# A projection with 512 instead of 256 moving columns per matmul, its end in halves

## The chip, the core and the metric

The kernel runs on one core of a Trainium2 chip. A core has TensorE (PE, matrix products; its loads of the stationary operand are listed as PEld), VectorE (DVE), ScalarE (ACT), GpSimd (POOL) and SyncE (SP, here the issuer of most DMA transfers). Operands lie in the on-chip memory SBUF, sums of matmuls in PSUM: 128 partitions, 8 banks of 512 float32 values each. The metric is the device time of one execution in microseconds (us). All numbers are float32; TensorE takes a weight and an activation as a pair of high and low parts each.

## The reference

A backbone with two layers over 512 tokens with 1024 features. Its last steps are what matters here: the channel mixer of the second layer, its gated residual, and the final RMSNorm.

```python
def conv_ffn(h, w_up, conv_w, conv_b, w_down):
    a, val = jnp.split(h @ w_up, 2, axis=-1)
    return (jax.nn.gelu(dwconv3(a, conv_w, conv_b), approximate=False) * val) @ w_down

def rms_norm(x, w):
    y = xf * lax.rsqrt(jnp.mean(xf * xf, axis=-1, keepdims=True) + EPS)
    return y * w

...
        x = x + gate_f[:, None, :] * conv_ffn(h, ...)
    return rms_norm(x, final_norm_w)
```

`w_down` is 2816 x 1024: 22 tiles of 128 rows (k = 0 to 21, FT = 22 in the kernel).

## The kernel before

The last projection computes, for four tiles i of 128 tokens, y = g @ w_down. The stationary operand is a 128 x 128 block of g (activations, high part gh or low part gl), the moving operand a k row block of the weights. Each product is three matmuls: gh with the high weights (line 1339), gl with the high weights (1340), gh with the low weights (1341). The 1024 output columns are done in four rounds j of 256 columns. In a round, four PSUM tiles, one for each token tile (tag acc, six banks), take the sums over all 22 k.

Weights come in loads of up to 8 k x 256 columns (1 MB) into two buffers (wraw). The class Weights converts them in sub-blocks of up to 4 k x 256 columns: ACT casts the high part (line 92), DVE subtracts for the low part (line 93), into three buffers each (whi, wlo). `get` hands out the next sub-block and converts one ahead; a cast waits until its buffer is free, that is until the matmuls of the sub-block three before it are done. In a round the sub-blocks begin at k0 = 0, 4, ..., 20; the last has 2 k.

The tiles of g lie in three pools: k = 0 to 5 in `gq` (high and low part side by side), the others in `zp` and `gp`.

After a round, `residual` adds the gated result to the residual stream xk: DVE multiplies the PSUM sum with the gate (line 1346) and adds it (1347), ACT squares it and sums the squares (1348). In the last round the last two sub-blocks are taken tile by tile: for each token tile the matmuls of both, its residual, then Ln and Exp for the inverse root (1370, 1371) and the scaling of the row: 256 columns with the final weights on DVE (1373), 512 on ACT (1374), 256 on DVE (1375). Two transfers write each tile out (1376 on ACT's queue, 1377 on SP's). Lines 1361 to 1363 do the first three quarters' share beforehand: the product with the final weights and the mean of the squares so far.

The order of an engine's instructions is not that of the program: the build reorders them, apart from pinned ones, by its own estimates of when each can run. It also adds all waits. The timelines show the order that runs. At the start of the stage 16 small matmuls that broadcast the gate (1324) and 32 transposes of the residual stream (1331) are mixed in.

The up-projection ahead of it (`group`) works with halves of a PSUM bank: `copy` (1176) reads one half of a bank while products for other banks, and then for the other half, follow. Its 512-column matmuls are on lines 288 to 290, with the weights stationary.

## Time and profile before

| | before |
|---|---|
| median of 3 runs | 1335.97 us (1333.49 to 1336.93) |
| profiled execution | 1333.99 us |
| its span | 1332.2 us |
| mean granted clock of TensorE | 0.995 |
| PE busy | 1304.5 us, 98% |
| PEld busy | 1147.6 us, 86% |
| DVE busy | 965.4 us, 72% |
| ACT busy | 625.2 us, 47% |
| instructions | 21229 |

The span is what the profile covers of the profiled execution; busy times are of its engines. A matmul's duration in a timeline (0.28 us for 256 columns) includes the passage through the array, which overlaps with the next one: the time that a matmul costs is the step from its start to the next start. A row of a timeline gives the start from the beginning of the span, the duration, engine, line and operation, output <- inputs, shapes, how many, and in brackets the idle time before it with what ended it.

### The profile page before, as it was taken

Reading aid. Unit: us, or ns where it says so; the run is one execution under the profiler, and the core shown is the slowest. Engines: PE = TensorE matmul, PEld = TensorE weight load, DVE = VectorE, ACT = ScalarE, POOL = GpSimd, SP = SyncE. Lnnn points to the kernel's source line nnn. Section 1 sums busy time; section 2 is a strip of 40 time slices with the busy share of each in tenths; the row PEclk is TensorE's granted clock in tenths of the full one; section 3 lists DMA queues with packets and bytes.
Section 4 is the critical chain, followed back from the end, with each engine's and each line's share of the span. In section 5 each row is a group of like instructions: output and inputs, shape, how many; then the busy total and the mean of one; then the engine's idle time right before and its main releaser. Section 6 shows DMA issues by size and latency. Waiting matters only on the chain. (4 is left out here: it accounts for less than half of the span.)

```text
span 1332.2 us, 21229 instructions
## 1 busy us (share of the span) xinstructions
PE 1304.5 (98%) x8456; PEld 1147.6 (86%) x8456; DVE 965.4 (72%) x1688; ACT 625.2 (47%) x1085; POOL 84.3 (6%) x87
## 2 busy tenths in 40 slices
PE   7999999999999999999999999999999999999997
PEld 4798888888779998889877898888999989899997
DVE  4668897887778878788766776667789897782333
ACT  4443445555545656565422253223456565663223
POOL 2204332311000000000000000000000000000000
PEclk9999999999999999999999999999999999999999
DMA  9842113674562122323466734555403423242231
GB/s 293 265 123 84 33 33 82 152 182 134 153 206 96 64 99 92 127 71 119 141 211 198 226 132 143 167 165 174 158 27 117 142 80 127 80 146 69 91 108 64
DMA packets 134995, 172.35 MB, mean 129 GB/s; under 512 B 14320, under 2 KB 103792, under 8 KB 129776
## 3 DMA queue, kind: packets, MB, share of 16 engines
q1 hardware_dynamic: 132896, 166.15, 39.3%
q10 hardware_dynamic: 2000, 4.85, 1.4%
q8 instruction: 66, 1.08, 0.3%
q14 instruction: 33, 0.27, 0.1%
HBM read 165.21 MB, written 2.10 MB: 126 GB/s over the span
## 5 line engine op out<-in xcount | busy, mean ns | idle before, releaser
L92 ACT CAST whi<-wraw 128x1024 fp32r<-128x1024 f32 (+1 forms) x122 | 124.1, 1021 | 280.8 <-PE pd L1340 70.4
L93 DVE TENSOR_TENSOR wlo<-wraw,whi 128x1024 fp32r<-128x1024 f32 (+1 forms) x122 | 145.2, 1192 | 107.7 <-ACT whi L92 107.1
L288 PE MATMUL p<-hf,whi 128*128 128x512 f32 (+1 forms) x640 | 215.4, 338 | 1.4 <-ACT whi L125 1.4
L290 PE MATMUL p<-hf,wlo 128*128 128x512 f32 (+1 forms) x640 | 214.6, 335 | 0.0
L289 PE MATMUL p<-hf,whi 128*128 128x512 f32 (+1 forms) x640 | 214.1, 335 | 0.0
L125 ACT CAST whi<-wraw 128x512 fp32r<-128x512 f32 (+1 forms) x160 | 113.0, 727 | 85.0 <-PE p L289 35.0
L290 PEld LDWEIGHTS p<-hf,wlo 128*128 128x128 f32 x640 | 120.1, 188 | 13.6
L288 PEld LDWEIGHTS p<-hf,whi 128*128 128x128 f32 x640 | 120.1, 188 | 12.3 <-ACT whi L125 1.6
L289 PEld LDWEIGHTS p<-hf,whi 128*128 128x128 f32 x640 | 120.1, 188 | 10.7
L126 DVE TENSOR_TENSOR wlo<-wraw,whi 128x512 fp32r<-128x512 f32 (+1 forms) x160 | 128.1, 817 | 0.9 <-ACT whi L125 0.5
L504 DVE SCALAR_TENSOR_TENSOR aa<-ar,sil,aa 128x512 f32<-128x512 f32 x140 | 104.8, 749 | 24.1 <-DMA ar<-in_ada_w_dram 21.8
L1339 PE MATMUL pd<-whi,g 128*128 128x256 f32 x352 | 98.2, 279 | 0.0
L1341 PE MATMUL pd<-wlo,g 128*128 128x256 f32 x352 | 98.1, 279 | 0.0
L1340 PE MATMUL pd<-whi,g 128*128 128x256 f32 x352 | 97.9, 278 | 0.0
L288 PE MATMUL pbd<-g,whi 128*128 128x512 f32 (+1 forms) x192 | 73.5, 383 | 0.0
L289 PE MATMUL pbd<-g,whi 128*128 128x512 f32 (+1 forms) x192 | 73.3, 382 | 0.0
L290 PE MATMUL pbd<-g,wlo 128*128 128x512 f32 (+1 forms) x192 | 73.1, 381 | 0.0
L288 PE MATMUL p<-T,whi 128*128 128x256 f32 x240 | 69.0, 288 | 0.0
L290 PE MATMUL p<-T,wlo 128*128 128x256 f32 x240 | 67.2, 280 | 0.0
L289 PE MATMUL p<-T,whi 128*128 128x256 f32 x240 | 67.2, 280 | 0.0
L1340 PEld LDWEIGHTS pd<-whi,g 128*128 128x128 f32 x352 | 66.3, 188 | 0.0
L1339 PEld LDWEIGHTS pd<-whi,g 128*128 128x128 f32 x352 | 66.1, 188 | 0.0
(679 smaller groups left out, 3296.3 us busy)
## 6 DMA issues: line engine op xcount, KB each, us to landing
ar<-in_ada_w_dram SPq DMA_DIRECT2D x160, 256.0 KB, 3.1
wraw<-in_upq_dram SPq DMA_DIRECT2D x40, 1024.0 KB, 4.8
wraw<-in_ffn_w_down_dram SPq DMA_DIRECT2D x16, 1024.0 KB, 5.3
wraw<-in_od_w_in_dram SPq DMA_DIRECT2D x12, 1024.0 KB, 5.6
wraw<-in_ev_w_in_dram SPq DMA_DIRECT2D x20, 512.0 KB, 5.2
araw<-in_ada_w_dram SPq DMA_DIRECT2D x16, 512.0 KB, 6.3
wraw<-in_ffn_w_down_dram SPq DMA_DIRECT2D x8, 768.0 KB, 4.7
wraw<-in_ev_w_out_dram SPq DMA_DIRECT2D x4, 1024.0 KB, 6.9
```

The lines of the kernel that those rows point to most:

```text
L92: self.nc.scalar.copy(hv, rv)
L93: self.pin(self.nc.vector.tensor_tensor(lv, rv, hv.bitcast(F32), ALU.subtract))
L125: self.nc.scalar.copy(hi, src)
L126: V.tensor_tensor(lo, src, hi.bitcast(F32), ALU.subtract)
L288: TE.matmul(o, wh, mh, start=start, stop=False, skip_group_check=True)
L289: TE.matmul(o, wh, ml, start=False, stop=False, skip_group_check=True)
L290: TE.matmul(o, wl, mh, start=False, stop=stop, skip_group_check=True)
L504: pin(V.scalar_tensor_tensor(self.acc[:], raw[:], sil[:, r, 0:1], self.acc[:], ALU.mult, ALU.add))
L1339: TE.matmul(o[i][:, 0:256], gh[:, ts], w[0][:, k - k0], start=k == 0, stop=False)
L1340: TE.matmul(o[i][:, 0:256], gl[:, ts], w[0][:, k - k0], start=False, stop=False)
L1341: TE.matmul(o[i][:, 0:256], gh[:, ts], w[1][:, k - k0], start=False, stop=k == FT - 1)
```

## The change

The last projection takes two rounds of 512 columns instead of four of 256. A load has up to 4 k x 512 columns, a sub-block 2 k x 512. A matmul moves 512 columns and fills a whole PSUM bank. In the second round the last two sub-blocks (k = 18 to 21) are done tile by tile and in two halves of 256 columns: for each half the matmuls of both sub-blocks, and then its residual; after the first half the sum of the squares so far and the product with the final weights for that half. `HALF` is the pair of slices 0:256 and 256:512.

```diff
-    for j in range(4):
-        plan += [wide(down[1], k0, k1, 256 * j) for k0, k1 in ((0, 8), (8, 16), (16, 22))]
+    for j in range(2):
+        plan += [([ktiled(down[1])[:, k0 : min(k0 + 4, FT), T * j : T * j + T]],
+                  [(0, s, s + 2, 0, T) for s in range(0, min(4, FT - k0), 2)]) for k0 in range(0, FT, 4)]
...
-    def down(o, w, i, k0):
+    def down(o, w, i, k0, c=slice(0, T)):
         ts = slice(i * P, (i + 1) * P)
-        for k in range(k0, min(k0 + 4, FT)):
+        for k in range(k0, k0 + 2):
             gh, gl = g[k]
-            TE.matmul(o[i][:, 0:256], gh[:, ts], w[0][:, k - k0], start=k == 0, stop=False)
-            TE.matmul(o[i][:, 0:256], gl[:, ts], w[0][:, k - k0], start=False, stop=False)
-            TE.matmul(o[i][:, 0:256], gh[:, ts], w[1][:, k - k0], start=False, stop=k == FT - 1)
+            TE.matmul(o[i][:, c], gh[:, ts], w[0][:, k - k0, c], start=k == 0, stop=False, skip_group_check=True)
+            TE.matmul(o[i][:, c], gl[:, ts], w[0][:, k - k0, c], start=False, stop=False, skip_group_check=True)
+            TE.matmul(o[i][:, c], gh[:, ts], w[1][:, k - k0, c], start=False, stop=k == FT - 1, skip_group_check=True)
...
+    def residual(o, i, j, c, n):
+        js = slice(j * T + c.start, j * T + c.stop)
+        t = fp.tile([P, T], F32, tag="t", name=f"yt{n}{i}", bufs=5)
+        V.tensor_tensor(t[:, c], o[i][:, c], gb[:, js], ALU.mult)
+        V.tensor_tensor(xk[i][:, js], xk[i][:, js], t[:, c], ALU.add)
+        S.activation(t[:, c], xk[i][:, js], AF.Square, accum_out=ss[:, i, n : n + 1])
...
-    subs = range(0, FT, 4)
-    for j in range(4):
+    subs = range(0, FT, 2)
+    for j in range(2):
...
-        V.tensor_tensor(xk[i][:, 0:768], xk[i][:, 0:768], fw[:, 0:768], ALU.mult)
-        V.tensor_reduce(ss[:, i, 4:5], ss[:, i, 0:3], axis=AX.X, op=ALU.add)
-        V.tensor_scalar(ss[:, i, 4:5], ss[:, i, 4:5], 1.0 / D, EPS, ALU.mult, ALU.add)
+        V.tensor_tensor(xk[i][:, 0:512], xk[i][:, 0:512], fw[:, 0:512], ALU.mult)
+        V.tensor_scalar(ss[:, i, 4:5], ss[:, i, 0:1], 1.0 / D, EPS, ALU.mult, ALU.add)
     w = [ws.get(), ws.get()]
     log_exp_table()
     for i in range(4):
-        for b in range(2):
-            down(o, w[b], i, subs[b - 2])
-        residual(o, i, 3)
-        S.activation(ss[:, i, 5:6], ss[:, i, 3:4], AF.Ln, scale=1.0 / D, bias=ss[:, i, 4:5])
+        for n, c in enumerate(HALF):
+            for b in range(2):
+                down(o, w[b], i, subs[b - 2], c)
+            residual(o, i, 1, c, 1 + n)
+            if n == 0:
+                V.scalar_tensor_tensor(ss[:, i, 4:5], ss[:, i, 1:2], 1.0 / D, ss[:, i, 4:5], ALU.mult, ALU.add)
+                V.tensor_tensor(xk[i][:, 512:768], xk[i][:, 512:768], fw[:, 512:768], ALU.mult)
+        S.activation(ss[:, i, 5:6], ss[:, i, 2:3], AF.Ln, scale=1.0 / D, bias=ss[:, i, 4:5])
```

## Rows read from the trace of the kernel before

**Rows 1.** The page, its first part: busy time of each engine, share of the span, instructions.

```profile
PE 1304.5 (98%) x8456; PEld 1147.6 (86%) x8456; DVE 965.4 (72%) x1688; ACT 625.2 (47%) x1085; POOL 84.3 (6%) x87
```

**Rows 2.** Groups by line and shape, 1160 to 1333 us: xcount | busy us, mean ns | idle before.

```profile
L1339 PE MATMUL pd<-whi,g 128*128 128x256 f32 x352 | 98.2, 279 | 0.0
...
L92 ACT CAST whi<-wraw 128x1024 fp32r<-128x1024 f32 x20 | 21.0, 1050 | 53.7 <-PE pd L1340 52.8 <-DMA wraw<-in_ffn_w_down_dram 0.9
...
L1363 DVE TENSOR_SCALAR ssf<-ssf 128x1 f32<-128x1 f32 x4 | 0.6, 149 | 0.0
```

**Rows 3.** The chain that ended last, in order of time: start us, us, what.

```profile
1327.73 0.48 DVE xk L1373
```

**Rows 4.** Timeline of PE, 256-column matmuls: start us, us, engine, line, operation.

```profile
1295.29 0.28 PE L1339 MATMUL pd<-whi,g 128*128 128x256 f32 x1
...
1299.61 0.28 PE L1339 MATMUL pd<-whi,g 128*128 128x256 f32 x1
...
1318.16 0.28 PE L1339 MATMUL pd<-whi,g 128*128 128x256 f32 x1
...
1324.85 0.28 PE L1341 MATMUL pd<-wlo,g 128*128 128x256 f32 x1
```

**Rows 5.** Busy time by stretch: sum PE, PEld, DVE, ACT, POOL, granted clock, DMA, GB/s.

```profile
1224.00:1228.00 4.00, 4.00 (x38) 4.00 (x37) 1.23 (x1) 1.05 (x1) 0.00 (x0) 1.00 0.55 190
1236.00:1240.00 4.00, 4.00 (x35) 4.00 (x34) 0.95 (x2) 0.96 (x5) 0.00 (x0) 1.00 0.33 118
```

**Rows 6.** Timeline of PE, 512-column matmuls of two other stages.

```profile
901.80 0.39 PE L288 MATMUL ppu<-hm,whi 128*128 128x512 f32 x1
...
905.70 0.40 PE L290 MATMUL ppu<-hm,wlo 128*128 128x512 f32 x1
...
1191.40 0.39 PE L288 MATMUL p<-hf,whi 128*128 128x512 f32 x1
...
1196.66 0.39 PE L290 MATMUL p<-hf,wlo 128*128 128x512 f32 x1
```

**Rows 7.** Timeline of PE where the last projection starts.

```profile
1199.97 0.47 PE L1324 MATMUL pgb<-dgb,ones 128*128 128x128 f32 x2
...
1202.56 0.61 PE L1324 MATMUL pgb<-dgb,ones 128*128 128x128 f32 x4
1202.92 0.36 PE L1339 MATMUL pd<-whi,g 128*128 128x256 f32 x1
...
1207.88 0.28 PE L1341 MATMUL pd<-wlo,g 128*128 128x256 f32 x1
```

**Rows 8.** Timeline of ACT in a group of the up-projection.

```profile
1180.30 0.35 ACT L1176 COPY R110r<-p 128x256 f32<-128x256 f32 x1
```

**Rows 9.** Timeline of PE beside it.

```profile
1180.78 0.31 PE L288 MATMUL p<-hf,whi 128*128 128x256 f32 x1
```

**Rows 10.** Timeline of DVE over the last two sub-blocks and behind.

```profile
1319.04 0.42 DVE L1346 TENSOR_TENSOR yt<-pd,gb 128x256 f32<-128x256 f32 x1 [6.19 <-PE pd L1341]
...
1321.07 0.48 DVE L1373 SCALAR_TENSOR_TENSOR xk<-xk,ssf,fw 128x256 f32<-128x256 f32 x1 [1.14 <-ACT ssf L1371]
1321.47 0.35 DVE L1375 TENSOR_SCALAR xk<-xk,ssf 128x256 f32<-128x256 f32 x1
...
1323.12 0.42 DVE L1346 TENSOR_TENSOR yt<-pd,gb 128x256 f32<-128x256 f32 x1 [0.51 <-PE pd L1341]
1323.75 0.49 DVE L1373 SCALAR_TENSOR_TENSOR xk<-xk,ssf,fw 128x256 f32<-128x256 f32 x1 [0.20 <-ACT ssf L1371]
...
1325.16 0.42 DVE L1346 TENSOR_TENSOR yt<-pd,gb 128x256 f32<-128x256 f32 x1 [0.33 <-PE pd L1341]
1325.62 0.43 DVE L1347 TENSOR_TENSOR xk<-xk,yt 128x256 f32<-128x256 f32 x1
```

**Rows 11.** Timeline of ACT behind the last matmul.

```profile
1326.00 0.72 ACT L1374 ACTIVATE xk<-xk,ssf 128x512 f32<-128x512 f32 x1
1326.63 0.40 ACT L1348 ACTIVATE yt<-xk 128x256 f32<-128x256 f32 x1
```

More of the change, by code (lines that the diff above doesn't have):

```diff
@@ L1333, in backbone @@
     ss = fp.tile([P, 4, 8], F32, tag="ss", name="ssf")
-    def down(o, w, i, k0):
+    def down(o, w, i, k0, c=slice(0, T)):
         ts = slice(i * P, (i + 1) * P)
-        for k in range(k0, min(k0 + 4, FT)):
+        for k in range(k0, k0 + 2):
             gh, gl = g[k]
-            TE.matmul(o[i][:, 0:256], gh[:, ts], w[0][:, k - k0], start=k == 0, stop=False)
-            TE.matmul(o[i][:, 0:256], gl[:, ts], w[0][:, k - k0], start=False, stop=False)
-            TE.matmul(o[i][:, 0:256], gh[:, ts], w[1][:, k - k0], start=False, stop=k == FT - 1)
-    def residual(o, i, j):
-        js = slice(j * 256, (j + 1) * 256)
-        t = fp.tile([P, 256], F32, tag="t", name=f"yt{j}{i}", bufs=5)
-        V.tensor_tensor(t[:], o[i][:, 0:256], gb[:, js], ALU.mult)
-        V.tensor_tensor(xk[i][:, js], xk[i][:, js], t[:], ALU.add)
-        S.activation(t[:], xk[i][:, js], AF.Square, accum_out=ss[:, i, j : j + 1])
-    subs = range(0, FT, 4)
-    for j in range(4):
+            TE.matmul(o[i][:, c], gh[:, ts], w[0][:, k - k0, c], start=k == 0, stop=False, skip_group_check=True)
[9 more added lines that the diff above has]
+    for j in range(2):
         o = [acc_t(f"pd1{j}{i}") for i in range(4)]
-        for k0 in subs if j < 3 else subs[:-2]:
+        for k0 in subs if j < 1 else subs[:-2]:
             w = ws.get()
@@ L1356, in backbone @@
                 down(o, w, i, k0)
-        if j < 3:
+        if j < 1:
             for i in range(4):
-                residual(o, i, j)
+                residual(o, i, j, slice(0, T), 0)
     for i in range(4):
-        V.tensor_tensor(xk[i][:, 0:768], xk[i][:, 0:768], fw[:, 0:768], ALU.mult)
-        V.tensor_reduce(ss[:, i, 4:5], ss[:, i, 0:3], axis=AX.X, op=ALU.add)
-        V.tensor_scalar(ss[:, i, 4:5], ss[:, i, 4:5], 1.0 / D, EPS, ALU.mult, ALU.add)
+        V.tensor_tensor(xk[i][:, 0:512], xk[i][:, 0:512], fw[:, 0:512], ALU.mult)
+        V.tensor_scalar(ss[:, i, 4:5], ss[:, i, 0:1], 1.0 / D, EPS, ALU.mult, ALU.add)
     w = [ws.get(), ws.get()]
```

## The prediction

> **What bounds the kernel now.** I read the share of busy time first, then the groups of lines, the chain that ended last, and then the timelines of the stretch that the change touches. TensorE (PE) is busy 98% of the span [rows 1]. The three matmul lines of the last projection, L1339 to L1341, have 352 instructions each, 1056 in all, and no idle time in front of them [rows 2]; so the stage is as long as its matmuls are, plus what runs behind the last one. The casts of its weights wait for PE (52.8 of 53.7 us of idle time), not the other way round [rows 2]: neither loads nor conversion bound it. The chain closes with the scaling of the fourth token tile on DVE at 1327.73 [rows 3], some 3 us behind the last matmul's start at 1324.85 [rows 4]. So two things count: time per moving column on PE, and the tail.
>
> The time per matmul has two levels. From 1318.16 to 1324.85 there are 59 steps of 0.1134 us; from 1295.29 to 1299.61 there are 36 steps of 0.120 us [rows 4]. DMA isn't the cause: a stretch with a DMA share of 0.55 has 38 matmuls in 4 us, one with 0.33 only 35, both at a granted clock of 1.00, the 2.4 GHz level [rows 5]. The two slow stretches lie just behind the start of the second and the fourth round. The slow steps last some 8 us of a round, as long as k = 0 to 5 take (72 x 0.120 = 8.6 us), and just these six tiles of the stationary operand lie in the pool `gq`. I take it that loading weights from there paces a 256-column matmul.
>
> **The change, part by part.**
>
> *Wider matmuls.* Removed: 1056 matmuls of 256 columns; 288 of them have k below 6: 288 x 0.120 + 768 x 0.1134 = 121.7 us. Added: 40 of the 44 pairs of round and k, each with 3 products for 4 tiles, are 480 matmuls of 512 columns, and the halves' 4 k x 3 x 4 x 2 are 96 of 256. The trace of before has no 512-column matmul with these operands (weights moving, activations stationary). The nearest rows are those of two other stages, with the operands exchanged: 17 steps in 3.90 us and 23 steps in 5.26 us, 0.2294 and 0.2287 us each [rows 6]. That is more than twice 0.1134, and less than twice 0.120. I take 0.2287: 480 x 0.2287 + 96 x 0.1134 = 120.7 us, a gain of 1.0 us. All of it comes from the slow k; the others lose a little. Bounds: if a matmul pays its columns at 2.4 GHz (256 columns are 0.1067 us) and a fixed 0.0067 us, which is what 0.1134 leaves, 512 columns take 0.2200 and the gain is 5.2 us. If the slow k stay slow at 2 x 0.120, the sum is 144 x 0.240 + 336 x 0.2287 + 10.9 = 122.3 us, a loss of 0.6 us.
>
> The Trainium skill (TensorE: Matmul & The Clock Gate, section "Back-to-back issue gap") gives a warm gap of N/2.4 + 2.5 ns, so 215.7 ns at 512 columns and 109.2 at 256. An estimate by that page makes the new stage 480 x 0.2157 + 96 x 0.1092 = 114.0 us, 7.6 us less than before, and a total of about 1328.2. The rows lie above it at both widths, by 4 and by 13 ns, so the trace doesn't bear it out here.
>
> *The start of the stage.* There 44 small matmuls (transposes and the broadcast of the gate) are mixed with the first ones of the projection: from 1199.97 to 1207.88 they and 16 of the projection's take 7.91 us. Four small ones take 0.36 us, from 1202.56 to 1202.92 [rows 7]. So 44 x 0.09 = 4.0 us, and the 16 take 3.9 us where 16 x 0.120 = 1.9 would do: 2.0 us go to changes of operation and to waits for the copies out of PSUM. A wider matmul in the same place does twice the work under the same wait. About half of the stretch has single ones in it, at most 9 x 0.11 = 1.0 us; I take 0.4 us of gain, with ends 0 and 1.0.
>
> *Weights.* Twelve loads stay twelve, with the same bytes. A sub-block is 2 k by 512 columns instead of 4 k by 256, so a conversion still has up to 1024 elements, and a sub-block lasts 24 x 0.2287 = 5.5 us against 48 x 0.1134 = 5.4. The short sub-blocks that ended each old round go. A 1024-wide cast takes 1.05 us [rows 2]; its subtraction on DVE is as wide. Nothing here is late; if the cover failed, one cast and one subtraction of some 2.3 us per sub-block would show as idle time of PE. At the one change of round left, 512-wide residuals stand in DVE's and ACT's queues ahead of at most one conversion: four tiles with two DVE operations of some 0.7 us (twice the columns of 0.42 [rows 10], less the fixed part) make 5.6 us, of which those of tile 3 alone, 1.4 us, and its square come behind the round's last matmul, with 5.5 us of matmuls to cover them. Two of the four new banks are free at once, and the other two wait for reads of tiles 0 and 1, which end their round 1.4 to 4 us earlier. I cost it at nothing.
>
> *The halves, a new wait.* In the last two sub-blocks a tile's first half is finished with 12 matmuls, L1346's successor reads it, and the second half's matmuls go on writing the same PSUM bank. Where before shows the same pattern, in the up-projection, the matmuls into one half of a bank start at 1180.78 [rows 9], behind the copy of the other half, which ends at 1180.30 + 0.35 [rows 8]: 0.13 us later. In the meantime PE does other products. No row shows one half read while PE writes the other. So I expect PE to wait. The price: after the last matmul's start at 1324.85 the next could start at 1324.96, but DVE's read starts only at 1325.16, takes 0.42 us [rows 4, 10], and 0.13 us follow: 1325.71, so 0.75 us for each wait. What is queued behind it on PE are the other tiles' matmuls; if they are put ahead, as in the up-projection, only tile 3 has nothing left to put ahead. I take one wait, +0.75 us; ends 0 and 4 x 0.75 = 3.0.
>
> The Trainium skill (PSUM — Partial Sum Buffer, section "PSUM bank collisions raise a hardware error") says that two engines must not touch the same bank and quadrant at once, even at different columns, and that the hardware doesn't arbitrate. By that rule the wait has to be there; it speaks against halves in one bank, and the trace agrees in the one place above.
>
> *The tail.* Per tile the halves add to DVE a product with the final weights (0.42), a second pair of multiply and add on the other half and a scalar step (0.15 [rows 2]). By durations a tile has 4 x 0.42 + 0.42 + 0.15 + 0.48 + 0.35 = 3.1 us on DVE [rows 2, 10], while PE takes 24 x 0.1134 = 2.7 us (18 x 0.1134 = 2.0 before). From a tile's first multiply to the end of its Exp are 2.03 us (1319.04 to 1321.07 [rows 10]). Before, tile 3's square could start when its add ended, at 1326.05, but ACT was scaling tile 2 until 1326.63 [rows 10, 11]: 0.58 us of lag. With 2.7 us between tiles that scaling ends about 0.7 us earlier relative to the last matmul, and the lag goes, unless DVE is behind by then, by up to 4 x (3.1 - 2.7) = 1.6 us. I take -0.5 us; ends -0.6 and +1.6.
>
> *Sum.* -1.0 - 0.4 + 0.75 - 0.5 = -1.15 us. The profiled execution took 1333.99 us, 1332.2 of them span; it would take 1332.8. It lies 2.0 us under the median of the three runs, 1335.97, which becomes 1334.8.
>
> **The rivals.**
>
> *512 columns cost only their columns and a small fixed part.* -5.2 instead of -1.0: 1335.97 - 5.35 = 1330.6. For it: with weights moving no 512-column row exists, and 256 columns run at 0.1134 with them. Against it: two stages agree at 0.229 [rows 6].
>
> *The slow k stay slow.* +0.6 instead of -1.0, so 1336.4: no gain on PE. For it: nothing but the unknown cause of the two levels.
>
> *PE waits at each of the four tiles.* +3.0 instead of +0.75: 1337.1. For it: the order in the program. Against it: PE's other work is put ahead in the up-projection.
>
> *DVE takes the tail's work in the order of the program* (slower than before). Then a tile's first half takes 2.1 us on DVE (multiply, add, wait for the square, scalar, product), its second 2.0 + 0.8: 4.9 us against PE's 2.7, and three tiles' lag of 2.2 make +6.6 behind the last matmul instead of -0.5: 1341.9. It decides once DVE holds a tile's scaling ahead of the next tile's first multiply. Against it: before, the third tile's multiply (1323.12) runs ahead of the second tile's scaling (1323.75) [rows 10], which isn't the order of the program.
>
> **How the numbers follow.** 0.3% of 1335.97 is 4.0 us, about what a measurement of this kernel can tell from no change. Forecast 0.56, 1334.8 (its own range 1332 to 1337); fixed part only 0.15, 1330.6; slow k 0.10, 1336.4; four waits 0.13, 1337.1; DVE in order 0.06, 1341.9. The range leaves out the last, and the lower part of the second: 1330.3 to 1338.3, the sum's ends and a micron of spread between runs. Faster by over 4.0 us: the second rival and a little of the forecast, 0.17. Slower: DVE in order and a little more, 0.07. Within: 0.76.
>
> **What would show it.** Steps between 512-column matmuls of the new lines: 0.229 bears me out, 0.220 the first rival, 0.240 at k below 6 the second. Idle time of PE released by DVE's first-half multiply: one of about 0.75 us or four. The chain behind the last matmul: 3.0 us to the last scaling or less, against 9 us with DVE in order. A PE idle at the change of round or for a cast would show the weights' cover wrong. The prediction fails if the moving operand's place in memory sets the rate of 512 columns.

## The result, and the profile after

The changed kernel takes 1338.26 us (median of 14 runs, 1334.33 to 1341.13), the kernel before 1335.44 in the runs beside it (14 runs, 1333.49 to 1337.81): ratio 1.0023, 95% interval 1.0014 to 1.0032. So it is slower by some 3 us; 1.2 us faster was forecast.

The single profiled execution took 1334.33 us with a span of 1332.5, which hides this: it is the fastest of the 14, and its last projection began 2.2 us earlier than in the profile of before (1194.72 against 1196.89), for reasons ahead of the change (in e6 below, which is alike up to there, it began at 1199.01). I therefore measure two stretches in every trace. The *stage* runs from the start of the first small matmul of the gate's broadcast (pgb) to the start of the last matmul of the projection, the *tail* from there to the end of the span.

| | before | after | difference |
|---|---|---|---|
| stage | 127.96 | 130.92 | +2.96 |
| tail | 7.3 | 6.9 | -0.4 |
| both | 135.3 | 137.8 | +2.5 |

First the page of after, then three groups by line and shape (1160 to 1333 us), which answer to [rows 1, 2].

```profile
PE 1303.7 (98%) x7976; PEld 1124.2 (84%) x7976; DVE 965.4 (72%) x1682; ACT 623.0 (47%) x1075; POOL 84.4 (6%) x87
```

```profile
L1340 PE MATMUL pd<-whi,g 128*128 128x512 f32 x160 | 63.5, 397 | 0.0
...
L92 ACT CAST whi<-wraw 128x1024 fp32r<-128x1024 f32 x22 | 23.1, 1050 | 74.7 <-PE pd L1341 74.1 <-DMA wraw<-in_ffn_w_down_dram 0.7
L1340 PE MATMUL pd<-whi,g 128*128 128x256 f32 x32 | 9.3, 290 | 0.7 <-DVE yt L1347 0.7
```

PE is as full as before, with fewer instructions, and the casts still wait for PE. The only new idle time that these groups show on PE is 0.7 us ahead of a 256-column matmul. The rest of the 2.96 us must be in the steps between matmuls. The timeline of PE in after shows it: the first and the last 512-column matmul behind the start of the stage, which answer to [rows 4, 6], then four changes of tile in the halves, then the last matmul.

```profile
1206.72 0.40 PE L1340 MATMUL pd<-whi,g 128*128 128x512 f32 x1
...
1312.87 0.40 PE L1342 MATMUL pd<-wlo,g 128*128 128x512 f32 x1
...
1314.92 0.28 PE L1341 MATMUL pd<-whi,g 128*128 128x256 f32 x1
1315.15 0.38 PE L1340 MATMUL pd<-whi,g 128*128 128x256 f32 x1
1315.37 0.29 PE L1341 MATMUL pd<-whi,g 128*128 128x256 f32 x1
...
1318.10 0.38 PE L1340 MATMUL pd<-whi,g 128*128 128x256 f32 x1
...
1321.19 0.39 PE L1340 MATMUL pd<-whi,g 128*128 128x256 f32 x1
...
1323.24 0.28 PE L1342 MATMUL pd<-wlo,g 128*128 128x256 f32 x1
1324.27 0.39 PE L1340 MATMUL pd<-whi,g 128*128 128x256 f32 x1 [0.75 <-DVE yt L1347]
...
1325.64 0.28 PE L1342 MATMUL pd<-wlo,g 128*128 128x256 f32 x1
```

From 1206.72 to 1312.87 there are 456 matmuls: 106.15 / 455 = 0.2333 us each, the same at every k, and with no gap at the change of round. In the halves most steps are 0.1134. Eight are longer, in four pairs, each at the start of a tile's second half: the step to its first matmul (0.22, 0.23, 0.26 and 1.03) and the step behind that (0.22 each time, as 1315.15 to 1315.37).

The accounting:

- Pace: 480 x 0.2333 + 96 x 0.1134 = 122.9 us against 121.7 before: +1.2.
- Halves: from 1313.11 to 1325.64 the 96 small matmuls take 12.53 us where 95 x 0.1134 = 10.77 would do: +1.75. Of it 1.03 - 0.11 = 0.92 lies in the long step, some 0.37 in the other three steps to a second half, some 0.43 in the four steps behind them, the rest in steps of 0.12.
- Start of the stage: stage less pace is 127.96 - 121.65 = 6.3 us before, and 130.92 - 122.87 - 1.75 = 6.3 after: 0.
- Tail: -0.4.

The pace's +1.2 is a loss at k from 6 on, 336 x (0.2333 - 2 x 0.1134) = 2.2 us, less a gain at k below 6, 144 x (2 x 0.120 - 0.2333) = 1.0. In all these make +2.5 us, the difference of the table and within the interval of the medians (1.9 to 4.3 us). DVE in the halves and the tail of after (answers to [rows 10]), and one load of a stationary operand, from PEld's timeline:

```profile
1314.67 0.42 DVE L1347 TENSOR_TENSOR yt<-pd,gb 128x256 f32<-128x256 f32 x1 [4.89 <-PE pd L1342]
...
1317.63 0.42 DVE L1347 TENSOR_TENSOR yt<-pd,gb 128x256 f32<-128x256 f32 x1
...
1319.92 0.42 DVE L1347 TENSOR_TENSOR yt<-pd,gb 128x256 f32<-128x256 f32 x1
...
1320.72 0.41 DVE L1347 TENSOR_TENSOR yt<-pd,gb 128x256 f32<-128x256 f32 x1
...
1323.01 0.41 DVE L1347 TENSOR_TENSOR yt<-pd,gb 128x256 f32<-128x256 f32 x1
...
1323.80 0.41 DVE L1347 TENSOR_TENSOR yt<-pd,gb 128x256 f32<-128x256 f32 x1
...
1326.09 0.42 DVE L1347 TENSOR_TENSOR yt<-pd,gb 128x256 f32<-128x256 f32 x1
...
1328.10 0.48 DVE L1377 SCALAR_TENSOR_TENSOR xk<-xk,ssf,fw 128x256 f32<-128x256 f32 x1 [1.14 <-ACT ssf L1375]
```

```profile
1321.19 0.19 PEld L1340 LDWEIGHTS pd<-whi,g 128*128 128x128 f32 x1 [0.18 <-DVE yt L1347]
```

The four first halves are read at 1314.67, 1317.63, 1320.72 and 1323.80, for 0.42 us each. These reads end at 1315.09, 1318.05, 1321.13 and 1324.21, and the first matmul of the same tile's second half starts at 1315.15, 1318.10, 1321.19 and 1324.27: 0.05 to 0.06 us behind the read, all four times. So PE waits for the bank at each of the four tiles. At the first three the wait is short, as five or six matmuls of the next tile are put ahead; the groups show it as no idle time of PE, since the matmul before is still passing through. The load of the stationary operand waits too. In the stream a load starts 0.11 us ahead of its matmul, behind a wait together with it (1321.19), and the step behind is 0.22 instead of 0.11.

The second halves of tiles 1 to 3 are read at 1319.92, 1323.01 and 1326.09, so DVE takes 3.09 us a tile (0.35 of it idle, for ACT's square, Ln and Exp), where 24 x 0.1134 are 2.7. The read of tile 3's first half, which releases PE at 1324.27, starts only at 1323.80, 0.56 us behind the start of the last matmul in front of it (1323.24).

### The profile page after: what moved, and what is told of

It reads as the page before. It is cut to its first block, busy times and chain, and to the rows that moved or that the text cites. A ratio compares the mean times of both kernels' runs of the same rounds, so it can differ in the third digit from the quotient of the medians.

```text
span 1332.5 us, 20251 instructions
## 1 busy us (share of the span) xinstructions
PE 1303.7 (98%) x7976; PEld 1124.2 (84%) x7976; DVE 965.4 (72%) x1682; ACT 623.0 (47%) x1075; POOL 84.4 (6%) x87
## 4 chain that ended last, share of the span: by engine, by line
PE 81%; DVE 10%; DMA 4%; ACT 3%; issue 2%; SPq 0%; DVEq 0%; ACTq 0%
PE p L289 11%; PE p L291 10%; PE p L290 10%; PE pd L1340 3%; PE pd L1341 3%; PE pd L1342 3%; DMA ar<-in_ada_w_dram 2%; PE pbd L291 2%; PE pbd L290 2%; PE pbd L289 2%; PE pbo L289 1%; PE ppc L289 1%; PE ppc L290 1%; PE ppc L291 1%; PE pbo L291 1%
## 5 line engine op out<-in xcount | busy, mean ns | idle before, releaser
L1340 PE MATMUL pd<-whi,g 128*128 128x512 f32 (+1 forms) x192 | 72.8, 379 | 0.7 <-DVE yt L1347 0.7
L1341 PE MATMUL pd<-whi,g 128*128 128x512 f32 (+1 forms) x192 | 72.2, 376 | 0.0
L1342 PE MATMUL pd<-wlo,g 128*128 128x512 f32 (+1 forms) x192 | 71.8, 376 | 0.0
L289 PEld LDWEIGHTS p<-T,whi 128*128 128x128 f32 x240 | 45.1, 188 | 3.9
L291 PEld LDWEIGHTS p<-T,wlo 128*128 128x128 f32 x240 | 45.2, 188 | 1.4
```

Of the source, the lines that this page charges most:

```text
L289: TE.matmul(o, wh, mh, start=start, stop=False, skip_group_check=True)
L291: TE.matmul(o, wl, mh, start=False, stop=stop, skip_group_check=True)
L1340: TE.matmul(o[i][:, c], gh[:, ts], w[0][:, k - k0, c], start=k == 0, stop=False, skip_group_check=True)
L1341: TE.matmul(o[i][:, c], gl[:, ts], w[0][:, k - k0, c], start=False, stop=False, skip_group_check=True)
L1342: TE.matmul(o[i][:, c], gh[:, ts], w[1][:, k - k0, c], start=False, stop=k == FT - 1, skip_group_check=True)
```

## The experiments

Two things had to be explained: why 512 columns take 0.2333 here and 0.2287 to 0.2294 in the other two stages [rows 6], and what the halves cost and give. Where a time stands without a number of runs or an interval, it is that of one execution; it says little by itself, and its trace is what is read.

### The halves: whole width at the end, and a bank for each half

*e6_whole_end* is after without halves: the last two sub-blocks tile by tile, 512 columns wide.

```diff
-        for n, c in enumerate(HALF):
-            for b in range(2):
-                down(o, w[b], i, subs[b - 2], c)
-            residual(o, i, 1, c, 1 + n)
...
+        for b in range(2):
+            down(o, w[b], i, subs[b - 2])
+        residual(o, i, 1, slice(0, T), 1)
...
```

> The changed kernel without the halves: the last two sub-blocks are taken tile by tile over all 512 columns, with one residual for each tile and one scaling of 512 columns on DVE. Theory: the waits for the bank (0.9 us of idle time and some 0.7 us at the changes of tile) go, the 96 matmuls of 256 columns (10.9 us) become 48 of 512 (11.2 us), so the stage goes from 130.9 to 129.6 us; the work behind the last matmul gets longer by a multiply, an add and a square of 512 instead of 256 columns, 0.7 to 0.8 us, so 6.9 becomes 7.6. Sum -0.6 us against the changed kernel, still some 2 us slower than before. Rival, the halves cost nothing on PE or save the tail more than that: slower than the changed kernel by up to 1 us.

Measured: 1338.32 us (7 runs), ratio to before 1.0030 (1.0015 to 1.0046); stage 129.35, tail 8.2, both 137.5 (after: 137.8). The stage is 1.57 us shorter, without a step over 0.24 behind 1211, and the tail 1.3 longer. The halves bring nothing: 0.3 us against them in the traces, no difference in the medians.

*e7_own_bank* is after, with tile 3's halves of the second round in two banks; tiles 0 to 2 keep one bank each.

```diff
...
         o = [acc_t(f"pd1{j}{i}") for i in range(4)]
+        if j:
+            o[3] = (o[3], acc_t("pd1b"))
```

> The changed kernel, but in the second round token tile 3 has two PSUM banks, one for each half of its columns, so its matmuls have 256 columns throughout the round (108 instead of 54 before the halves). Theory, PE's idle time of 0.91 us in the changed kernel (step of 1.03 us less 0.12) comes from the bank that DVE still reads: it is gone. The 54 wide steps of 0.233 become 108 of 0.1134 or 0.120 for k below 6: 0.2 us less. The stage (start of the first small matmul to start of the last matmul), 130.9 us, becomes 129.8; the tail behind the last matmul (6.9 us) grows by as much as DVE or ACT are late with tile 2, at most 1 us. Rival, PE waits for the tail's DVE work as such: the idle time stays.

Measured: 1339.2 us. The second half of tile 3 carries the name pd1b. First PE: the start of tile 2's second half, and the last matmul of tile 3's. Then DVE: the read of tile 2's first half, and what runs behind the last matmul.

```profile
1326.04 0.38 PE L1342 MATMUL pd<-whi,g 128*128 128x256 f32 x1
...
1329.46 0.28 PE L1344 MATMUL pd1b<-wlo,g 128*128 128x256 f32 x1
```

```profile
1325.57 0.42 DVE L1350 TENSOR_TENSOR yt<-pd,gb 128x256 f32<-128x256 f32 x1
...
1330.95 0.42 DVE L1350 TENSOR_TENSOR yt<-pd1b,gb 128x256 f32<-128x256 f32 x1
...
1332.96 0.49 DVE L1382 SCALAR_TENSOR_TENSOR xk<-xk,ssf,fw 128x256 f32<-128x256 f32 x1 [1.14 <-ACT ssf L1380]
```

Tile 3's wait is gone, with both of its long steps, and the stage takes 129.8 us, 1.2 less. Tiles 0 to 2, which keep one bank, still have theirs: tile 2's second half starts at 1326.04, 0.05 behind the end of the read of its first half, and the steps of 0.22 to 0.25 are there at these three tiles alone. But DVE reads tile 3's second half 1.49 us behind the start of its last matmul (0.45 in after), the tail takes 8.0, and both make 137.7 against 137.8. So tile 3's wait for the bank and DVE's lag are one lag, which is paid in the one place or in the other. The pace of DVE and ACT, 3.09 us a tile, sets the end: from DVE's read of tile 0's second half to its last scaling there are 11.27 us in after and 11.28 in e7.

### The pace: order, pools, pairs

*e1_order_512* (after) and *e2_order_256* (before) exchange the second and the third product, so that gh stays stationary for two matmuls in a row (shown for before; in after the same two lines).

```diff
-            TE.matmul(o[i][:, 0:256], gl[:, ts], w[0][:, k - k0], start=False, stop=False)
-            TE.matmul(o[i][:, 0:256], gh[:, ts], w[1][:, k - k0], start=False, stop=k == FT - 1)
+            TE.matmul(o[i][:, 0:256], gh[:, ts], w[1][:, k - k0], start=False, stop=False)
+            TE.matmul(o[i][:, 0:256], gl[:, ts], w[0][:, k - k0], start=False, stop=k == FT - 1)
```

> The changed kernel with one edit: of the three products of a k the two with gh as stationary operand follow each other (gh w-high, gh w-low, gl w-high) instead of gh, gl, gh. The steps of 512-column matmuls in this stage measured 0.2332 us, while stages with the weights stationary (stationary operand high, high, low) have 0.2287. Theory A, the repeated stationary operand makes the difference: the step falls from 0.2332 to about 0.2287, the stage (start of the first small matmul to start of the last matmul) from 130.9 to 128.8 us. Theory B, the moving operand or its place makes it: the step stays at 0.233 and the stage at 130.9.

> The kernel before with the same edit: gh w-high, gh w-low, gl w-high. Theory A, a repeated stationary operand is cheaper: the steps of 0.120 for k = 0 to 5 and of 0.1134 for the others fall, to about 0.113 and below. Theory B, place alone: 0.120 and 0.1134 stay, the stage (first small matmul to last matmul) stays at 128.0 us.

Measured: 1339.83 and 1333.3 us; steps 0.2333 in the one, 0.120 (k below 6) and 0.1133 in the other, stages 130.96 and 127.95. Nothing moves: the order isn't it.

*e3_pool_256* is before with k = 4 to 9 of g in `gq`, and k = 0 to 3 in `zp`.

```diff
-        if f < 6:
-            t = gq.tile([P, 2, T], F32R, tag=f"q{f}", name=f"g{l}{f}")
+        if 4 * l <= f < 4 * l + 6:
+            t = gq.tile([P, 2, T], F32R, tag=f"q{f - 4 * l}", name=f"g{l}{f}")
...
```

> The kernel before with the high and low parts of g for k = 4 to 9 in the pool gq and k = 0 to 3 in zp (before: k = 0 to 5 in gq, 6 to 9 in zp). My theory of the two levels, loads of the stationary operand from gq pace a 256-column matmul: in each round the first 4 k (48 matmuls, 5.4 us) now step at 0.1134, k = 4 to 9 (72 matmuls) at 0.120, the rest at 0.1134. Rival, the start of a round is slow (residuals on DVE and ACT, fresh banks): the first 8 to 9 us of a round stay at 0.120. The stage stays at 128.0 us in both.

Measured: 1335.67 us, stage 128.18. The busy time by stretch, with PE's matmuls in the first brackets, of before and then of e3; the first stretch lies behind the start of a round in before, the second some 6 us later:

```profile
1234.00:1239.00 5.00, 5.00 (x44) 5.00 (x43) 2.95 (x7) 2.62 (x9) 0.00 (x0) 1.00 0.50 157
...
1241.00:1250.00 9.00, 9.00 (x81) 9.00 (x80) 2.20 (x2) 1.05 (x1) 0.00 (x0) 1.00 0.35 117
```

```profile
1234.00:1239.00 5.00, 5.00 (x47) 5.00 (x46) 4.66 (x10) 2.57 (x8) 0.00 (x0) 1.00 0.51 150
...
1241.00:1250.00 9.00, 9.00 (x78) 9.00 (x77) 2.45 (x2) 2.10 (x2) 0.00 (x0) 1.00 0.38 118
```

The slow stretch moves with the tiles in `gq`, as the prediction had it. The trace of before has it matmul by matmul, too: where a sub-block mixes k = 4, 5 (`gq`) with k = 6, 7 (`zp`), six steps of 0.120 alternate with six of 0.113 (1240.81 to 1241.53 to 1242.21).

*e4_moving_gq* is after, with three weight sub-blocks of the second round in buffers of `gq`.

```diff
+            if j == 1 and k0 == 8:
+                ws.spare = [(gq, f"q{2 * n}", f"q{2 * n + 1}") for n in range(3)]
```

> The changed kernel, but in the second round, once k = 0 to 5 are used up, the high and low parts of three sub-blocks of weights (72 matmuls of 512 columns) are written into the six tiles of the pool gq instead of the pool wp. Theory C, the 0.2332 us come from where the moving operand lies (pool wp): for these 72 matmuls, some 17 us in the second round, the step is another, about 0.2287. Theory D, they come from the pairing of operands as such, or from the other operand: it stays at 0.233 there.

Measured: 1337.71 us, stage 131.00, 0.2333 throughout. The pool of the moving operand alone is not it either, with `gp` stationary.

*e5_pairs* replaces factors in the second round of after: for some k the stationary or the moving operand is another tile. It computes other sums, so only its pace is read.

```diff
...
+            if second and k0 in (6, 10, 12):
+                w0, w1 = g[{6: 16, 10: 18, 12: 2}[k0] + k - k0]
+            if second and k0 in (8, 10):
+                sh, sl = w[0][:, k - k0, ts], w[1][:, k - k0, ts]
+            if second and k0 == 14:
+                sh, sl = (t[:, ts] for t in g[4 + k - k0])
...
```

> The changed kernel with other operands in five sub-blocks of the second round, so that its sums are those of other factors; number and shape of the matmuls stay. For k = 6, 7 the moving operand is tiles of g (pool gp) instead of weights, stationary g as ever. For k = 8, 9 both operands are weights (pool wp). For k = 10, 11 stationary weights (wp), moving g (gp): the arrangement of the other projections. For k = 12, 13 stationary g (gp), moving g from the pool gq. For k = 14, 15 stationary g from gq, moving weights. Theory S, the stationary operand's place sets the step: 0.2287 us for k = 8 to 11, 0.233 for the others. Theory M, the moving operand sets it: 0.2287 for k = 6, 7, 10 to 13, 0.233 for 8, 9, 14, 15. Theory P, only the pair of weights stationary and g moving is cheap: 0.2287 for k = 10, 11 alone.

Measured: 1334.78 us, stage 130.69. First and last matmul by pair, in the timeline of PE: k = 6, 7 from its eighth matmul on (the steps before it, 0.224 to 0.236, lead over), k = 8, 9, k = 10, 11, and k = 12, 13.

```profile
1281.85 0.39 PE L1349 MATMUL pd<-g,g 128*128 128x512 f32 x1
...
1285.48 0.39 PE L1350 MATMUL pd<-g,g 128*128 128x512 f32 x1
1285.71 0.39 PE L1348 MATMUL pd<-whi 128*128 128x512 f32 x1
...
1290.93 0.39 PE L1350 MATMUL pd<-wlo,whi 128*128 128x512 f32 x1
1291.16 0.40 PE L1348 MATMUL pd<-g,whi 128*128 128x512 f32 x1
...
1296.44 0.40 PE L1350 MATMUL pd<-g,whi 128*128 128x512 f32 x1
1296.68 0.39 PE L1348 MATMUL pd<-g,g 128*128 128x512 f32 x1
...
1302.04 0.39 PE L1350 MATMUL pd<-g,g 128*128 128x512 f32 x1
```

Over 16 and three times 23 steps these are 0.2269, 0.2270, 0.2296 and 0.2330 us. `zp` stationary and `gp` moving, and weights against weights, are fast; weights stationary and `gp` moving, and `gp` stationary and `gq` moving, are slower. It is neither operand's pool by itself: it is the pair.

### A use of what was known by then: the width by the pool

*e8_width_by_pool* is after without halves, with 512 columns only for k below 6 and 256 for the others (in the second round in two passes with the tail of before).

```diff
...
-                down(o, w, i, k0)
+                down(o, w, i, k0, 2, both if k0 < 6 else HALF)
...
```

> A version of two rounds of 512 columns in which only k = 0 to 5 (stationary tiles in gq, 0.120 us per 256 columns) have matmuls of 512 columns, and the others 256; in the second round the first 256 columns are finished before the second 256, and the last 8 k are taken tile by tile at 256 columns, no halves of a bank. Theory, the width decides by 0.233 against 2 x 0.1134 or 2 x 0.120: matmuls 144 x 0.2333 + 768 x 0.1134 = 120.7 us, 1.0 us less than before and 2.2 less than the changed kernel, no wait on PE: stage 127.0 us; the tail has 2.7 us of matmuls per tile, so the lag of tile 3's square goes, 7.35 becomes 6.9. Total 1.4 us faster than before, ratio 0.999. Rival, changing width or rounds costs elsewhere: stage 128 us or more, ratio 1.000 or above.

Measured: 1333.9 us (11 runs) against 1334.85: ratio 0.9995 (0.9982 to 1.0007). Stage 126.96, tail 6.8: 1.6 us less than before in the traces, of it 1.0 in the stage, as 144 x (2 x 0.120 - 0.2333) wants it, the rest in the tail. It can't be told from no change by the medians.

### The distance of the pair in memory

What tells these pairs apart is where the tiles start in a partition. The build's layout has whi and wlo at 192 modulo 256 bytes, `zp` and `gp` at 0, `gq` and the pool `fp` at 96. Call *distance* the start of the moving operand less that of the stationary one, modulo 256. In e5 the four pairs above have 0, 0, 64 and 96. Pads change the distances without touching the work. In the order of the diff: 64 bytes move the weights, 64 more `zp` and `gp`, and 96 bytes in the pool of the residual stream move `gq` and `fp`.

```diff
+    cpad = cp.tile([P, 16], F32, name="cpad")
...
-            red = ap_.tile([P, 16], F32, tag="ared", name=f"ad{self.n}", bufs=1)
+            red = ap_.tile([P, 32], F32, tag="ared", name=f"ad{self.n}", bufs=1)[:, 0:16]
...
+    xpad = xp.tile([P, 24], F32, name="xpad")
...
```

*e9_align_before* and *e10_align_after* have all three (weights and `gq` at 0, `zp` and `gp` at 128), *e11_align_wp* is after with the first two.

> The kernel before with three paddings and nothing else: 64 bytes in the pool cp, 64 in ap_, 96 in xp. By them every tile that TensorE reads starts at a multiple of 128 bytes in its partition. In the kernel before, the converted weights (wp) start at 64 more than such a multiple, gq, fp and xp at 96 more, zp, yp, gp at a multiple. Theory A: a matmul is slow where the stationary and the moving operand start at different places modulo 128 (0.2332 us for weights against g, 0.120 per 256 columns for gq against wp), and fast where they agree (0.227 us in the runs with both operands in wp, or one in zp and one in gp). Then all steps fall to 0.2267 and 0.1134, in all stages: the stage of the last projection from 128.0 to 126.0 us, and some 20 us of the whole program's PE steps go, of which the parts bound by PE keep most: total 1318 to 1325 us, ratio 0.985 to 0.993. Rival B, the pair of pools or the data set the step: unchanged, ratio 1.000.

> The changed kernel with the same three paddings. Theory A: its 512-column steps fall from 0.2332 to 0.2267, which is just twice 0.1134, so width no longer matters, and against the padded kernel before there remain the waits at the halves (1.75 us) less the shorter tail (0.5): 1.2 us slower than that, ratio to it about 1.001; total 1319 to 1326 us. Rival B: 0.2332 stays, ratio to the kernel before 1.0023.

> The changed kernel with the paddings in cp and ap_ alone: wp, zp, yp and gp start at a multiple of 128 bytes, gq, fp and xp at 96 more as before. Theory A: for k = 0 to 5 (stationary g in gq) the step of 512 columns stays at 0.233, for the others it falls to 0.2267; the stage is 130.9 - 336 x 0.0066 = 128.7 us. Rival B: 0.2332 for all k, stage 130.9.

Measured: 1349.17, 1346.98 and 1347.04 us; ratios of the first two to before 1.0104 (1.0088 to 1.0120) and 1.0089 (1.0068 to 1.0109). Starts at a multiple of 128 bytes are no remedy: 256 columns take 0.120 (k below 6) and 0.1187, 512 columns 0.2267 and 0.2324, and in e11 0.234 and 0.2324. The projection's stage accounts for 3.9 us of e9's 14.6; the rest lies ahead of it, where other matmuls have other distances too, but I didn't follow it there.

*e14_equal_after* and *e15_equal_before* widen the second pad so that all operands start at 0.

```diff
-            red = ap_.tile([P, 16], F32, tag="ared", name=f"ad{self.n}", bufs=1)
+            red = ap_.tile([P, 64], F32, tag="ared", name=f"ad{self.n}", bufs=1)[:, 0:16]
```

> The changed kernel with paddings of 64 bytes in cp, 192 in ap_ and 96 in xp: weights (wp), zp, yp, gp, gq and fp all start at a multiple of 256 bytes, distance 0 everywhere. Theory A2: its 512-column steps fall from 0.2333 to 0.2267 for all k, the 256-column ones of the halves rise from 0.1134 to 0.120; stage 130.9 - 3.2 + 0.6 = 128.3 us. In the other stages 512 columns gain 0.002 us each and 256 columns lose 0.0024, some 2 us more in all. Total 1336 to 1340 us. Rival B2: 0.2333 stays for k from 6 on.

> The kernel before with the same paddings as the padded changed kernel, all distances 0. Theory A2: all its 256-column steps are 0.120, so the stage of the last projection is 1056 x 0.120 + 6.3 = 133.0 us, 4.7 more than the padded changed kernel's: with these places the change is a gain of some 5 us, ratio of the padded changed kernel to this one 0.996, where it was 1.0023 with the old places. Total 1341 to 1345 us. Rival B2: 0.1134 stays for k from 6 on and the stage at 126 to 128 us.

Measured: after with these pads 1337.99 us (10 runs), before with them 1344.13 (4 runs), ratios to the kernel before 1.0019 (1.0008 to 1.0030) and 1.0061 (1.0046 to 1.0076). Stages 128.04 and 132.96. So with these places the same change brings 6.1 us (0.9954, from the medians; 5.0 of it in the stage and the tail) where with the original ones it costs 3. All steps are 0.2267, or 0.120. Nothing but places differs, so the places set the pace. With these places neither kernel is faster than before with its own.

*e12_gq_place* is before with the 96-byte pad alone, *e13_places* before with 224 bytes there and 128 more in `gq`; in both all k have distance 192, where before has its 0.1134.

```diff
+    xpad = xp.tile([P, 24], F32, name="xpad")
...
```

```diff
+    xpad = xp.tile([P, 56], F32, name="xpad")
...
+    qpad = gq.tile([P, 32], F32, tag="qpad", name="qpad")
...
```

> The kernel before with one padding of 96 bytes in xp, which moves gq and fp down by 96 bytes. Theory A2: the step depends on the distance from the stationary to the moving operand's start modulo 256 bytes. From the runs so far, for 512 and 256 columns: distance 0 0.2267 and 0.120; 64 0.2287 and 0.1176; 96 0.2333 and 0.120; 128 0.2322 and 0.1188; 192 0.2333 and 0.1134. Here the only pair of the last projection that changes is gq against the weights, from 96 to 192: its steps fall from 0.120 to 0.1134, the stage of the last projection from 128.0 to 126.0 us; the first layer's down-projection gains some 0.5 us for the same tiles; ratio 0.998. Rival B2, only a common residue or the pools as such count: 0.120 stays for k = 0 to 5.

> The kernel before with paddings of 224 bytes in xp and 128 in gq: gq at a multiple of 256 bytes as in the run with one padding, and fp, which holds the moving operand T of the up-projections, at a multiple plus 128. Theory A2: besides the 2.0 us of the last projection, the up-projections' 720 matmuls with T (stationary weights at 192, T at 128: distance 192 instead of 160) step at 0.1134 instead of 0.1176, 3.0 us less. Total 5 to 6 us faster than before, ratio 0.996. Rival B2: no change at T, ratio 0.998 to 1.000.

Measured: 1334.14 us, ratio 0.9988 (0.9975 to 1.0002), and 1335.0, 0.9997 (0.9981 to 1.0012). The stages are 130.89 and 126.24: e13 has 0.1133 throughout, but e12 has 0.1177, though k = 6 to 21 lie where before has them. The up-projection in front, whose moving operand `T` lies in `fp`, has the distance 192 too in e13, but its 256-column matmuls with `T` stay at the 0.1177 that they have in before (35 steps in 4.12 us). So the distance fails to tell the pace here twice. Three more runs:

*e16_gq_again* is e12 once more, *e17_gq_order* adds the change of e3 to it, *e18_gq_alone* has the 96 bytes inside `gq`, so that `fp` stays where before has it.

```diff
+    qpad = gq.tile([P, 24], F32, tag="qpad", name="qpad")
...
```

> The kernel before with the pad of 96 bytes ahead of gq once more, unchanged. In the first look at it every step of the projection was 0.1177 us, the stage 130.9 us, though k = 6 to 21 have all their operands where the kernel before has them, with 0.1134. If the step is a property of the build (places and order), it is 0.1177 again and the stage 130.9. If it can change from one execution to the next, it may be 0.1134 (stage 126.2, as with the pads of 224 and 128 bytes) or something else.

> The same pad, and k = 4 to 9 of g in gq, k = 0 to 3 in zp, so that a round begins with tiles that lie where the kernel before has its fast ones. If the step depends on the places of the pair at work alone, k = 0 to 3 and 10 to 21 have 0.1134 as in the kernel before, or all have 0.1177 as in the last run with this pad. If a step once slow stays slow until something sets it back, k = 0 to 3 of the first round have 0.1134, k = 4 to 9 then 0.1177, and everything behind them 0.1177 too.

> The kernel before with the pad of 96 bytes inside gq instead of ahead of the pools: gq starts where it did in the last two runs, the pool fp (which the projection's matmuls don't read) stays where the kernel before has it. If the place of gq makes the 0.1177, all steps are 0.1177 and the stage takes 130.9 us. If the place of fp does, or chance, the steps are 0.1134 by the table of distances and the stage takes 126.2 us.

Measured: 1334.08, 1336.12 and 1333.73 us (before 1334.41), stages 130.75, 130.75 and 126.26. Busy time from 1220 to 1300 us, of e14, e15, e16, e17 and e18; the count in the first brackets is PE's matmuls, the column behind POOL's the granted clock:

```profile
1220.00:1300.00 80.00, 80.00 (x355) 66.27 (x354) 25.84 (x31) 17.61 (x23) 0.00 (x0) 1.00 0.27 89
```

```profile
1220.00:1300.00 80.00, 80.00 (x669) 80.00 (x669) 21.94 (x31) 17.87 (x31) 0.00 (x0) 1.00 0.28 90
```

```profile
1220.00:1300.00 80.00, 80.00 (x681) 80.00 (x680) 27.69 (x45) 20.02 (x39) 0.00 (x0) 1.00 0.30 96
```

```profile
1220.00:1300.00 80.00, 80.00 (x681) 80.00 (x681) 26.36 (x41) 20.65 (x40) 0.00 (x0) 1.00 0.30 96
```

```profile
1220.00:1300.00 80.00, 80.00 (x708) 80.00 (x707) 27.76 (x46) 20.71 (x40) 0.00 (x0) 1.00 0.30 96
```

At the same clock of 1.00 PE starts 355 matmuls of 512 columns (after has 344), and 669, 681, 681 or 708 of 256. Behind its start the projection has the 0.1177 in all three executions with the pad ahead of the pools (e12, e16, e17), whatever tiles begin the round, and not in e18, where only `fp` is put back. That looks like a property of the build. But the traces of e12 and e16, one build, differ where the projection starts. In both these are 18 steps between its first matmuls, up to where the gate's broadcast interrupts them; first e16, then e12:

```profile
1195.27 0.28 PE L1341 MATMUL pd<-whi,g 128*128 128x256 f32 x1
...
1197.31 0.28 PE L1341 MATMUL pd<-whi,g 128*128 128x256 f32 x1
```

```profile
1195.93 0.28 PE L1341 MATMUL pd<-whi,g 128*128 128x256 f32 x1
...
1198.05 0.28 PE L1341 MATMUL pd<-whi,g 128*128 128x256 f32 x1
```

They take 0.1133 us in e16 and 0.1178 in e12; behind the interruption both have 0.1177 to the end. In the up-projection of e16, the same 36 matmuls with `T` of two groups, one after the other:

```profile
1037.63 0.28 PE L288 MATMUL p<-T,whi 128*128 128x256 f32 x1
...
1041.59 0.28 PE L290 MATMUL p<-T,wlo 128*128 128x256 f32 x1
...
1058.45 0.28 PE L288 MATMUL p<-T,whi 128*128 128x256 f32 x1
...
1062.57 0.28 PE L290 MATMUL p<-T,wlo 128*128 128x256 f32 x1
```

The 35 steps take 0.113 us in the one group and 0.1177 in the other, and in e12 the second of these groups has 0.113, too (1060.05 to 1064.01). So in these builds a stretch of 256-column matmuls takes one of two paces and keeps it to its end; another group, or another execution, can take the other. It isn't carried over from the up-projection either, whose last stretch with `T` has 0.1177 in e16 and 0.1134 in e12. Whether the place of `fp` decides that there are two paces, or e18's single execution had the fast one by chance, is not shown.

## Why the prediction was wrong

*What bounds the kernel* held: PE is full before and after, casts and loads stay hidden, and the stage is as long as its matmuls plus the tail. A median of 14 runs and the two stretches of the traces agree on that.

*Wider matmuls* is the step that failed: "I take 0.2287". It is 0.2333, and 480 x 0.0046 = 2.2 us turn -1.0 into +1.2, the gain into a loss. The mistake lay in the choice of the row. The rows of the other stages [rows 6] have weights stationary at 192 and activations moving at 0, a distance of 64; e5 puts such pairs into this stage and finds 0.2296. The new matmuls have distances of 192 and 96, where 512 columns take 0.2333; and for most k before sits at the distance where 256 columns are at their best. The stated lower and upper ends were 0.220 for all k, and 0.240 for the slow ones with 0.2287 for the rest: neither end let the fast k lose as much as they did. Its last sentence came near the cause, the moving operand's place, but without a price and without the stationary operand. Twice the step of before was at hand as a bound, 2 x 0.1134 = 0.2268 and 2 x 0.120 = 0.240, and the measured step lies between.

The reading that `gq` paces 256 columns was right as to where (e3), but not as to why: with the pads of e13 and e18 `gq` is read at 0.1133. So it hangs on where the tiles lie, not on which pool they are in. That it is the loads from there that set the pace, no run shows.

The Trainium skill (TensorE: Matmul & The Clock Gate, section "Back-to-back issue gap") has N/2.4 + 2.5 ns, 215.8 ns at 512 columns and 109.2 at 256, for a matmul by itself, and some 131 ns at 512 for a stream of loads and matmuls; the prediction took the former for a stream's. No run here agrees with either: the fastest steps are 0.2267 and 0.1133 us, and the same count of columns has several paces at a granted clock of 1.00.

*The start of the stage*: -0.4 forecast, 0 measured, the end that the prediction gave. *Weights and the change of round* at nothing: right, no step of PE there is longer than 0.24 us.

*The halves*: +0.75 forecast for one wait, at tile 3; +1.75 measured, in four. This is the second step that failed. Other tiles' matmuls are put ahead as forecast, but at tiles 0 to 2 only five or six of them, 0.57 to 0.68 us, while DVE's read ends 0.73 to 0.88 us behind the start of the half's last matmul. At tile 3 the read starts 0.56 us behind that matmul, not 0.31 as in before, and ends 0.05 ahead of the next one, not 0.13: 0.92. The step behind each wait, 0.11 more, had no term. The Trainium skill (PSUM — Partial Sum Buffer, section "PSUM bank collisions raise a hardware error") says that two engines must not be in the same bank and quadrant at once, even at different columns. The build puts in the wait that this asks for, and the trace has it: tile 3's second half starts 0.05 us behind DVE's read of the other half, and with a bank of its own (e7) it doesn't wait. Whether the chip needs it no run here shows.

*The tail*: -0.5 forecast, -0.4 measured. ACT's lag goes as forecast: from DVE's last read to the last scaling there are 2.57 us in before (1325.16 to 1327.73) and 2.01 in after. But the forecast took the tail and the wait for two things. By e7 they are one: DVE's lag shows in the tail (8.0 us) when tile 3 doesn't wait, and the forecast's figure fits because PE's wait takes it up. That is luck. So is the 3.1 us that it has for DVE's work on a tile: it adds durations, which overlap, and the trace's 3.09 hold 0.35 of waiting for ACT.

*The rivals*: 0.220 and 0.240 appear nowhere; PE does wait four times, as the third has it, but three of the waits are short, and all cost 1.75, not 3.0; DVE takes the next tile's multiply ahead of the scaling (1323.80 ahead of 1325.02). The larger part of the loss, the pace at k from 6 on, is in none of the rivals.

In sum: -1.0 - 0.4 + 0.75 - 0.5 = -1.15 was forecast, +1.2 + 0 + 1.75 - 0.4 = +2.5 is what the traces show. The time, 1338.26, lies at the upper edge of the range, 1338.3, by luck: the bounds of the halves and the tail were wide enough, while the pace was bounded at a loss of 0.6 us.

## What to carry to other kernels

In this kernel the step of a back-to-back matmul depends on where the pair of operands lies in memory, with 3 to 6 per cent between places; a duration from another stage with the same shape is a row of another pair, so bound a change of width by twice the old step, too. Where a kernel is bound by PE, read the steps by stretch, list where its stationary and moving tiles start, and try a pad: it is a cheap experiment, though none of those here made the whole kernel measurably faster. And before you split work into halves to shorten a tail, add up the round of the engines that take each half, with their waits for each other: if it is longer per tile than PE's, the gain comes back as a wait. A wait needn't show as idle time; look for long steps, and for what ended just before them.

## What the runs showed of the hardware

The steps by distance (moving less stationary start, modulo 256 bytes), in us:

| distance | 512 columns | 256 columns |
|---|---|---|
| 0 | 0.2267 (e5, e10, e14) | 0.120 (e9, e15) |
| 64 | 0.2287 to 0.2296 ([rows 6], e5) | 0.118 (up-projection of before), 0.1133 or 0.1177 (of e12, e16) |
| 96 | 0.2333 (after, e4, e5) | 0.120 (before) |
| 128 | 0.2324 (e10, e11) | 0.1187 (e9) |
| 160 | 0.234 (e11) | 0.1177 (up-projection of before) |
| 192 | 0.2333 (after) | 0.1134 (before, e13, e18) or 0.1177 (e12, e16, e17; up-projection of e13) |

Unexpected is that the two widths rank two of the places the other way round: a distance of 0 is the best for 512 columns and among the worst for 256, 192 the best for 256 and among the worst for 512. So one change of width costs 3 us with one layout and brings 6 with another. The table is a description, not a mechanism: the two values at 192 and at 64, and e12 against e16, one build, show that the distance of the pair isn't all there is. At 512 columns no pair has turned up at two such paces: after's layout has 0.2333 in after, e1, e4, e6 and e7. What picks the pace of a stretch stays open.

A wait for a PSUM bank costs PE two long steps: the one that waits, whose matmul starts 0.05 us behind the end of DVE's read, and 0.22 instead of 0.11 us for the one behind it (after, four times).
